# Loading the middle weight columns of a fused q/k/v product as fp32 through SyncE and rounding them on GpSimd

## The chip, the cores and the metric

The kernel runs on one core of one Trainium2 chip. The time is the device time of one execution in microseconds (us); the figure that counts is the median over the runs. Besides the times there is one profiled execution, whose trace gives the start and the duration of every instruction and of the DMA packets.

## The reference

```python
x = np.random.randn(16, 512, 768).astype(np.float32)
w_qkv = np.random.randn(768, 3 * 768).astype(np.float32)

qkv = np.matmul(x, w_qkv)            # (16, 512, 2304)
q, k, v = qkv[..., :768], qkv[..., 768:1536], qkv[..., 1536:]
return np.stack([q, k, v], axis=0)   # (3, 16, 512, 768), fp32
```

So 8192 rows of x, 768 long, are multiplied by one 768 x 2304 matrix w, and the result is written as three matrices.

## The kernel before

**Tiling.** The rows of x are cut into 32 pairs of two 128-row tiles (`p` counts pairs, `r` the row tile in a pair). The columns of w are cut into two groups of 1024 (`q` = 0 and 1), each of two blocks of 512 (`c`), and 256 columns between the groups, the remaining columns (`REM`, at `R_OFF` = 1024). K = 768 is split into six slices `j` of 128, three in each half (`KH` = 3).

**Two ways to multiply.** A pair and a column group make a two by two block product: two row tiles, two halves of K, two column blocks. For most pairs it is done with seven products instead of eight (`do(u, 1)` to `do(u, 7)`, matmuls at L257): products 1 and 2 take bf16 operands (`xb`, `b1`), products 3 to 7 take sums of x blocks (`sums_x`, L224 to L228) and sums of w blocks (`sum_w`, L123) in fp32r. The first two pairs are done in the plain way, in bf16 and slice by slice (`block`, L500), because then PE can begin as soon as the first slices of w are there. The remaining columns are always plain bf16 products against `w_rem[0]` (K slices 0 to 2) and `w_rem[1]` (slices 3 to 5), 128x256 each.

**The order at the start.** The engines' programs are written out by hand (`manual_schedule`): what is called first stands first on its engine. SyncE (SP) issues, in this order, x of pairs 0 and 1, the twelve slices of w for q = 0, the eight parts of x of pair 2 (`load_x_rows(2)`, L141, four for each row tile), and then the blocks of w for q = 1 (`load_blocks(1, 0)` and `(1, 1)`). SP uses eight completion semaphores in turn, so each of its transfers is issued only when the eighth before it has landed. The 256 remaining columns are loaded by GpSimd (POOL): `hold` makes it wait, with a one-element copy, until a slice of w has landed; then it issues two DMAs (L461) that read fp32 and write bf16 into `w_rem[0]` and `w_rem[1]`; a second `hold` waits for pair 2's first row tile.

PE does `block(0, 0)` and `block(0, 1)` for pairs 0 and 1, then `rems_by_halves` (L338, 24 matmuls: both pairs with the first half of `w_rem`, then both pairs with the second half), and then pair 2: products 1 and 2 (L257), the remaining columns of pair 2 (`rem(2)`, L312), products 5 and 6 (`middle`), and from there `block(1, 0)` with products 7, 3 and 4 of pair 2 between its slices.

Pair 2 gets ready as follows. DVE transposes x in four steps (L157), two for each row tile, after it has made the second sum of w blocks (`sum_w(0, 2)`, L123). ACT rounds each row tile to bf16 (`round_row`, L211) among its copies out of PSUM: `late[0]` to `late[3]` (L490) copy the four results of `block(0, 1)`, `rems[...]()` (L327) copy the remaining columns of pairs 0 and 1, `evacuate` (L266) copies product 1. POOL rounds a block of w into `b22[0]` (L581), which product 3 reads. After that ACT rounds w for q = 1 (`cast_j`, L476).

From pair 3 on, each group of pairs repeats the same pattern to the end.

Of the kernel before, what the change touches and what calls it, by code (L numbers as in the profile page):

```python
# [10 lines left out]
def kernel(  # L11
# [20 lines left out]
    nc = tc.nc  # L32
    P = 128
# [5 lines left out]
    KT = K // P  # L39
    KH = KT // 2  # L40
    KC = K // 4
    NP = M // (2 * P)
    CB = 512
    REM = N3 - 4 * CB
    Q_OFF = (0, 2 * CB + REM)
    R_OFF = 2 * CB
    fp32 = mybir.dt.float32
# [3 lines left out]
    add = mybir.AluOpType.add  # L51
# [10 lines left out]
    o_pool = ctx.enter_context(tc.tile_pool(name="o", bufs=5))  # L62
# [9 lines left out]
    ps_pool = ctx.enter_context(tc.tile_pool(name="ps", bufs=8, space=bass.MemoryType.PSUM))  # L72
# [5 lines left out]
    w_rem = [w_pool.tile([P, KH, REM], bf16, name="w_rem0"), None]  # L78
# [13 lines left out]
    def load_w(dst, j0, nj, off, cols):  # L92
        rows = w_qkv.rearrange("(p j) n -> p j n", j=KT)
        nc.sync.dma_start(dst, rows[:, j0:j0 + nj, off:off + cols])  # L94

    stage = {}
# [18 lines left out]
    def sum_w(q, n):  # L115
        t1, t2, t3, t4 = ts[q]
        o, in0, in1 = {
            1: (t1, stage[q, 0, 1], stage[q, 0, 0]),
            2: (t2, stage[q, 1, 1], t1),
            3: (t3, stage[q, 1, 1], stage[q, 0, 1]),  # L120
            4: (t4, stage[q, 1, 0], t2),
        }[n]
        nc.vector.tensor_tensor(o, in0, in1, op=sub)  # L123

    xin, xf, xb, sr = {}, {}, {}, {}
# [8 lines left out]
    def load_x_rows(p, parts=range(8)):  # L134
        if p not in xin:
            xin[p] = xin_pool.tile([P, 2 * P // G, KC], fp32, name="xin")
        rows = x_flat[p * 2 * P:(p + 1) * 2 * P, :].rearrange("(g b) k -> b g k", b=G)
        for n in parts:
            r, i = divmod(n, 4)
            gs = slice(r * P // G, (r + 1) * P // G)  # L140
            nc.sync.dma_start(  # L141
                xin[p][i * G:(i + 1) * G, gs], rows[:, gs, i * KC:(i + 1) * KC]
            )
# [60 lines left out]
    act, dve = nc.scalar, nc.vector  # L204

    def round_row(p, r, eng):
        n = slice(r * P, (r + 1) * P)
        if r == 0:
            xb[p] = xb_pool.tile([P, KT, 2 * P], bf16, name="xb", tag="xb")
        if eng is act:  # L210
            eng.activation(xb[p][:, :, n], xf[p][:, :, n], ident)  # L211
        else:
            eng.tensor_copy(out=xb[p][:, :, n], in_=xf[p][:, :, n])
# [25 lines left out]
    def quad(p, q, pool=o_pool, tag="o"):  # L239
        u = Quad()  # L240
        u.p, u.q = p, q
        u.o = pool.tile([P, 2, 2 * CB], fp32, name="o", tag=tag)
        u.x = u.y = u.z = None
        return u

    def product(u, n, ps, start):
        t1, t2, t3, t4 = ts[u.q]
        if n <= 2:
            h = (n - 1) * KH
            lhs = [xb[u.p][:, h + j, :P] for j in range(KH)]  # L250
            rhs = [b1[u.q][:, h + j, :] for j in range(KH)]
        else:
            k, t = {3: (4, b22[u.q][:]), 4: (0, t4), 5: (1, t1), 6: (2, t2), 7: (3, t3)}[n]
            lhs = [sr[u.p][k][:, j, :] for j in range(KH)]
            rhs = [t[:, j, :] for j in range(KH)]
        for j in range(KH):
            nc.tensor.matmul(  # L257
                ps[:], lhs[j], rhs[j],
                start=(start and j == 0), stop=(j == KH - 1), skip_group_check=True,
            )  # L260

    def bank():
        return ps_pool.tile([P, CB], fp32, name="ps")

    def evacuate(u):
        nc.scalar.activation(u.o[:, 0, :CB], u.x[:], ident)  # L266

    def do(u, n, out=True):
        c11, c12 = u.o[:, 0, :CB], u.o[:, 0, CB:]
        c21, c22 = u.o[:, 1, :CB], u.o[:, 1, CB:]  # L270
        if n == 1:
            u.x = bank()
            product(u, 1, u.x, True)
            if out:
                evacuate(u)
        elif n == 2:
            u.z = bank()
            product(u, 2, u.z, True)
            nc.vector.tensor_tensor(c11, c11, u.z[:], op=add)  # L279
        elif n == 6:  # L280
            product(u, 6, u.x, False)
            nc.scalar.activation(c12, u.x[:], ident)  # L282
        elif n == 5:
            u.y = bank()
            product(u, 5, u.y, True)
        elif n == 7:
            product(u, 7, u.x, False)
            nc.scalar.activation(c22, u.x[:], ident)  # L288
            nc.vector.tensor_tensor(c22, c22, u.y[:], op=add)  # L289
        elif n == 4:  # L290
            product(u, 4, u.x, False)
            nc.scalar.activation(c21, u.x[:], ident)  # L292
        elif n == 3:
            product(u, 3, u.y, False)
            nc.vector.tensor_tensor(c12, c12, u.y[:], op=add)  # L295
# [27 lines left out]
    def rem_copied(p, ps, eng=nc.sync):  # L323

        def copied():
            o = or_pool.tile([P, 2, REM], fp32, name="orem")
            act.activation(o[:], ps[:], ident)  # L327
            return lambda: eng.dma_start(rows_of(1, p, R_OFF - H, R_OFF - H + REM), o[:])

        return copied  # L330

    def rems_by_halves(pairs):
        banks = [ps_pool.tile([P, 2, REM], fp32, name="ps") for _ in pairs]
        for h in range(2):
            for p, ps in zip(pairs, banks):
                for r in range(2):
                    for j in range(KH):
                        nc.tensor.matmul(  # L338
                            ps[:, r, :], xb[p][:, h * KH + j, r * P:(r + 1) * P],
                            w_rem[h][:, j, :], start=(h == 0 and r == 0 and j == 0),  # L340
                            stop=(h == 1 and j == KH - 1), skip_group_check=True,
                        )
        return [rem_copied(p, ps) for p, ps in zip(pairs, banks)]

    def two(a, b, early, ends=(), turns=()):

# [93 lines left out]
    ND = 2  # L440
# [8 lines left out]
    load_row(1, 1)  # L449
    load_slices(0, [(j, 1, 0, CB) for j in range(1, KT)])  # L450
    load_slices(1, [(j, 1, 0, CB) for j in range(KT)])
    load_x_rows(2)

    def hold(src):
        mark = m_pool.tile([P, 1], fp32, name="mark")
        nc.gpsimd.tensor_copy(out=mark[:], in_=src)

    hold(stage[0, 1, 0][:, KH - 1, :1])
    for h in range(2):
        rows = w_qkv.rearrange("(p j) n -> p j n", j=KT)[:, h * KH:(h + 1) * KH]  # L460
        nc.gpsimd.dma_start(w_rem[h][:], rows[:, :, R_OFF:R_OFF + REM])  # L461
    hold(xin[2][:, 0, :1])
    load_blocks(1, 0)

    one = nc.const_aps.tensor(1.0, [P, CB], bf16)
# [16 lines left out]
    def block(q, c, w, groups, between={}):  # L482

        ps = {}
        late = []

        def finish(n):
            p, r = divmod(n, 2)
            u = quads[p, q]
            act.activation(u.o[:, r, c * CB:(c + 1) * CB], ps[n][:], ident)  # L490

        for i, (js, tiles, *cols) in enumerate(groups):
            cols = cols[0] if cols else slice(0, CB)
            for n in tiles:
                p, r = divmod(n, 2)
                fresh = n not in ps
                if fresh:
                    ps[n] = bank()
                for j in js:
                    nc.tensor.matmul(  # L500
                        ps[n][:, cols], xb[p][:, j, r * P:(r + 1) * P], w[:, j, cols],
                        start=(fresh and j == 0), stop=(j == KT - 1), skip_group_check=True,
                    )
                if KT - 1 not in js:
                    continue
                if (p, q) not in quads:
                    quads[p, q] = quad(p, q)
                late.append(lambda n=n: finish(n))
            between.get(i, lambda: None)()
        return late  # L510
# [4 lines left out]
    def copy_y(u):  # L515
        act.activation(u.o[:, 1, CB:], u.y[:], ident)

    def middle(u, order=(6, 5)):
        for n in order:
            do(u, n)  # L520
            if n == 5:
                copy_y(u)
# [51 lines left out]
    for f in late0:  # L574
# [3 lines left out]
    cast_j(0, 1, bt, 4, act)  # L578
    cast_j(0, 1, bt, 5, act)
    sum_w(0, 2)  # L580
    nc.gpsimd.tensor_copy(out=b22[0][:], in_=stage[0, 1, 1])  # L581
    late = block(
        0, 1, bt,
        [((j, ), range(4)) for j in range(KH + 1)] + [(range(KH + 1, KT), range(4))],
    )
    rems = rems_by_halves(range(2))
    transpose(2, 4)

    late[0]()
    late[1]()  # L590
    round_row(2, 0, act)
    rem_stores = [rems[0]()]
    late[2]()
    late[3]()
    round_row(2, 1, act)
    rem_stores.append(rems[1]())
    load_blocks(1, 1)
    for store in rem_stores:
        store()
# [8 lines left out]
    sum_w(0, 3)  # L608
    sums[3](dve)
    sums[4](dve)  # L610

    u = quad(2, 0)
    do(u, 1)
    do(u, 2)
    cast_j(1, 0, b1[1], 0)
    rem2 = rem(2)
    cast_j(1, 0, b1[1], 1)
    middle(u, (5, 6))
    store2 = []

    def rest():
# [126 lines left out]
```

## Time and profile before

| | |
|---|---|
| median of 3 runs | 359.55 us (359.37 to 359.61) |
| the profiled execution, its own time | 359.58 us |
| its span in the trace | 357.7 us |
| busy share of the span | PE 98%, DVE 65%, ACT 52%, POOL 51% |
| DMA | 107.72 MB, mean 301 GB/s over the span |
| DMAs issued by GpSimd | 800 packets, 0.39 MB, both in the first 20 us |

The span runs from the first to the last instruction of the trace; the 1.9 us by which the execution's own time is longer lie around it. In the views, a line such as "18.96 2.62 PE ps L338 x24" gives a start and a length in us, the engine, the tile written, the line of the kernel and the number of instructions. Some matmul records are missing from a trace, so that a group of six can stand as x5. The span that a line gives to a group of matmuls includes the pipeline's run-out of the last one; what one costs is seen from the distance between starts.

### The profile page before, as it was taken

What the parts mean: (1) busy time and instruction counts of PE and PEld (TensorE: products, weight loads), DVE (VectorE), ACT (ScalarE), POOL (GpSimd) and SP (SyncE); (2) the same over time, 40 slices, a digit from 0 to 9 for tenths busy, and PEclk for the clock granted to TensorE, in tenths of its full rate; (3) what the DMA queues carried; (4) which work ended last, traced back from release to release, by engine and by line L of the source; (5) the groups of instructions that cost most, each with busy time, mean ns of one, the idle gap of its engine ahead of it and who ended that gap; (6) DMA issues with size and microseconds to landing.
All of it is one profiled execution on the core that took longest, in us unless ns stands there. A gap on an engine that the chain in (4) does not pass through costs nothing.

```text
span 357.7 us, 5219 instructions
## 1 busy us (share of the span) xinstructions
PE 350.9 (98%) x1755; PEld 253.2 (71%) x1775; DVE 233.1 (65%) x250; ACT 185.1 (52%) x317; POOL 182.6 (51%) x193
## 2 busy tenths in 40 slices
PE   8999999999999999999999999999999999999995
PEld 3465777767768687776867768687776867768774
DVE  3889985887574676647577574676647577544643
ACT  5489545454545454544554545454544554545453
POOL 0228759481754717357371754717357371754420
PEclk9999999999999999999999999999999999999999
DMA  7999999999899898979989899898989989856667
GB/s 284 340 385 333 321 313 406 384 343 328 342 275 339 283 262 324 277 276 309 302 310 247 324 275 339 274 271 331 258 288 316 295 320 239 322 209 234 265 247 254
DMA packets 81963, 107.72 MB, mean 301 GB/s; under 512 B 5264, under 2 KB 62096, under 8 KB 81936
## 3 DMA queue, kind: packets, MB, share of 16 engines
q1 hardware_dynamic: 74288, 101.86, 85.8%
q10 hardware_dynamic: 6848, 5.13, 5.8%
q0 software_dynamic: 800, 0.39, 0.8%
q8 instruction: 14, 0.23, 0.3%
q14 instruction: 13, 0.11, 0.1%
HBM read 32.26 MB, written 75.50 MB: 301 GB/s over the span
## 4 chain that ended last, share of the span: by engine, by line
PE 95%; DMA 1%; ACT 1%; SPq 1%; issue 1%; ACTq 0%; DVE 0%
PE ps L257 79%; PE ps L312 11%; PE ps L500 4%; DMA st<-in_w_qkv_dram 1%; PE ps L338 1%; ACT o L292 1%; SPq L172 0%; ACTq L399 0%; SPq L94 0%; ACT orem L413 0%; ACT both L476 0%; DVE b L478 0%; ACTq L415 0%; ACTq L413 0%
## 5 line engine op out<-in xcount | busy, mean ns | idle before, releaser
L257 PE MATMUL ps<-t,z 128*128 128x512 f32 x366 | 98.3, 390 | 0.0
L257 PE MATMUL ps<-t,s 128*128 128x512 f32 x366 | 97.2, 400 | 0.0
L157 DVE STREAM_TRANSPOSE xf<-xin 128x1536 f32<-128x1536 f32 (+2 forms) x37 | 91.6, 2484 | 2.0 <-DMA xin<-in_x_dram 1.2
L224 POOL TENSOR_TENSOR s<-xf 128x384 fp32r<-128x384 f32 x29 | 29.5, 1018 | 117.9 <-PE ps L257 116.5
L257 PE MATMUL ps<-b,xb 128*128 128x512 bf16 x347 | 83.3, 379 | 1.2
L257 PEld LDWEIGHTS ps<-t,s 128*128 128x128 f32 x366 | 68.7, 188 | 15.9
L257 PEld LDWEIGHTS ps<-t,z 128*128 128x128 f32 x366 | 68.6, 188 | 14.7 <-ACT o L282 0.3
L289 DVE TENSOR_TENSOR o<-o,ps 128x512 f32<-128x512 f32 x56 | 38.4, 685 | 58.7 <-ACT o L288 58.7
L257 PEld LDWEIGHTS <-xb 128*128 128x128 bf16 x366 | 34.3, 98 | 37.5 <-issue 5.0
L279 DVE TENSOR_TENSOR o<-o,ps 128x512 f32<-128x512 f32 x61 | 39.4, 676 | 31.2 <-PE ps L257 28.8
L288 ACT ACTIVATE o<-ps 128x512 f32<-128x512 f32 x56 | 33.5, 598 | 42.7 <-PE ps L257 42.7
L295 DVE TENSOR_TENSOR o<-o,ps 128x512 f32<-128x512 f32 x61 | 41.6, 685 | 20.2 <-PE ps L257 18.9
L282 ACT ACTIVATE o<-ps 128x512 f32<-128x512 f32 x61 | 36.6, 600 | 34.8 <-PE ps L257 32.1
L266 ACT ACTIVATE o<-ps 128x512 f32<-128x512 f32 x61 | 36.4, 598 | 31.3 <-PE ps L257 18.3
L257 PE MATMUL ps<-b,s 128*128 128x512 f32 x183 | 51.2, 390 | 0.0
L292 ACT ACTIVATE o<-ps 128x512 f32<-128x512 f32 x61 | 36.5, 598 | 26.7 <-PE ps L257 23.6
L202 POOL CAST xb<-xf 128x1536 bf16<-128x1536 f32 x28 | 41.0, 1465 | 12.4 <-DVE xf L157 12.4
L312 PE MATMUL ps<-w_rem,xb 128*128 128x256 bf16 x360 | 44.4, 273 | 0.0
L312 PEld LDWEIGHTS <-xb 128*128 128x128 bf16 x360 | 35.0, 98 | 10.8 <-issue 0.5
L257 PEld LDWEIGHTS ps<-b,s 128*128 128x128 f32 x183 | 34.3, 188 | 7.3
L226 POOL TENSOR_TENSOR z<-xf 128x384 fp32r<-128x384 f32 x29 | 29.3, 1011 | 3.9 <-PE ps L257 3.9
L228 POOL TENSOR_TENSOR s<-xf,s 128x384 fp32r<-128x384 f32 x29 | 30.7, 1059 | 0.1
(54 smaller groups left out, 171.3 us busy)
## 6 DMA issues: line engine op xcount, KB each, us to landing
out_dram<-o SPq DMA_DIRECT2D x62, 768.0 KB, 4.6
xin<-in_x_dram SPq DMA_DIRECT2D x90, 192.0 KB, 6.0
out_dram<-o SPq DMA_DIRECT2D x65, 256.0 KB, 3.7
out_dram<-orem SPq DMA_DIRECT2D x31, 256.0 KB, 5.6
xin<-in_x_dram ACTq DMA_DIRECT2D x22, 192.0 KB, 6.7
st<-in_w_qkv_dram SPq DMA_DIRECT2D x11, 256.0 KB, 5.2
st<-in_w_qkv_dram SPq DMA_DIRECT2D x3, 768.0 KB, 10.1
xin<-in_x_dram SPq DMA_DIRECT2D x4, 384.0 KB, 4.2
```

Of the source, the lines that this page charges most:

```text
L157: lambda g=g: nc.vector.transpose(turned[:, g:g + n], rows[:, g:g + n])
L202: nc.gpsimd.tensor_copy(out=xb[p][:], in_=t[:])
L228: 4: lambda g: g.tensor_tensor(s[4], a12, s[2], op=sub),
L257: nc.tensor.matmul(ps[:], lhs[j], rhs[j], start=(start and j == 0), stop=(j == KH - 1), skip_group_check=True,)
L266: nc.scalar.activation(u.o[:, 0, :CB], u.x[:], ident)
L279: nc.vector.tensor_tensor(c11, c11, u.z[:], op=add)
L282: nc.scalar.activation(c12, u.x[:], ident)
L288: nc.scalar.activation(c22, u.x[:], ident)
L289: nc.vector.tensor_tensor(c22, c22, u.y[:], op=add)
L292: nc.scalar.activation(c21, u.x[:], ident)
L295: nc.vector.tensor_tensor(c12, c12, u.y[:], op=add)
L312: nc.tensor.matmul(ps, xb[p][:, j, r * P:(r + 1) * P], w_rem[j // KH][:, j % KH, :], start=(j == 0), stop=(j == KT - 1), skip_group_check= ...
```

## The change

The two DMAs of GpSimd and both of their `hold`s go. A staging tile `st_rem` (128 x 6 x 256 fp32, from the pool of the output tiles, `o`) takes the remaining columns as fp32. SP loads it in two halves, each right behind the four parts of one row tile of pair 2. GpSimd rounds each half into `w_rem` (`round_rem`), the first before and the second behind the rounding into `b22[0]`. On PE the products of pairs 0 and 1 with the remaining columns stand in two parts: those with the first half where they were, those with the second half behind products 1 and 2 of pair 2, which therefore come earlier. ACT copies the remaining columns of both pairs together after `round_row(2, 1)`, and `evacuate` comes ahead of that. `middle(u)` now takes product 6 first and 5 second.

```diff
-    def rems_by_halves(pairs):
-        banks = [ps_pool.tile([P, 2, REM], fp32, name="ps") for _ in pairs]
-        for h in range(2):
-            for p, ps in zip(pairs, banks):
...
+    def rems_half(pairs, banks, h):
+        for p, ps in zip(pairs, banks):
+            for r in range(2):
+                for j in range(KH):
+                    nc.tensor.matmul(
+                        ps[:, r, :], xb[p][:, h * KH + j, r * P:(r + 1) * P],
+                        w_rem[h][:, j, :], start=(h == 0 and r == 0 and j == 0),
+                        stop=(h == 1 and j == KH - 1), skip_group_check=True,
+                    )
...
-    load_x_rows(2)
+    st_rem = o_pool.tile([P, KT, REM], fp32, name="str", tag="o")
+    for h in range(2):
+        n = slice(h * KH, (h + 1) * KH)
+        load_x_rows(2, range(4 * h, 4 * h + 4))
+        load_w(st_rem[:, n], h * KH, KH, R_OFF, REM)
+
+    def round_rem(h):
+        n = slice(h * KH, (h + 1) * KH)
+        nc.gpsimd.tensor_copy(out=w_rem[h][:], in_=st_rem[:, n])
...
-    hold(stage[0, 1, 0][:, KH - 1, :1])
-    for h in range(2):
-        rows = w_qkv.rearrange("(p j) n -> p j n", j=KT)[:, h * KH:(h + 1) * KH]
-        nc.gpsimd.dma_start(w_rem[h][:], rows[:, :, R_OFF:R_OFF + REM])
-    hold(xin[2][:, 0, :1])
     load_blocks(1, 0)
...
     sum_w(0, 2)
+    round_rem(0)
     nc.gpsimd.tensor_copy(out=b22[0][:], in_=stage[0, 1, 1])
+    round_rem(1)
...
-    rems = rems_by_halves(range(2))
+    banks = [ps_pool.tile([P, 2, REM], fp32, name="ps") for _ in range(ND)]
+    rems_half(range(ND), banks, 0)
     transpose(2, 4)
 
     late[0]()
     late[1]()
     round_row(2, 0, act)
-    rem_stores = [rems[0]()]
     late[2]()
     late[3]()
+    u = quad(2, 0)
+    u.x, u.z = bank(), bank()
+    product(u, 1, u.x, True)
+    product(u, 2, u.z, True)
+    rems_half(range(ND), banks, 1)
+    evacuate(u)
     round_row(2, 1, act)
-    rem_stores.append(rems[1]())
+    rem_stores = [rem_copied(p, ps)() for p, ps in enumerate(banks)]
     load_blocks(1, 1)
...
-
-    u = quad(2, 0)
-    do(u, 1)
-    do(u, 2)
+    c11 = u.o[:, 0, :CB]
+    dve.tensor_tensor(c11, c11, u.z[:], op=add)
+
     cast_j(1, 0, b1[1], 0)
     rem2 = rem(2)
     cast_j(1, 0, b1[1], 1)
-    middle(u, (5, 6))
+    middle(u)
```

More of the change, by code (lines that the diff above doesn't have):

```diff
@@ L330, in rem_copied @@
         return copied
-    def rems_by_halves(pairs):
-        banks = [ps_pool.tile([P, 2, REM], fp32, name="ps") for _ in pairs]
-        for h in range(2):
-            for p, ps in zip(pairs, banks):
[L336 to L343, printed above, removed]
+    def rems_half(pairs, banks, h):
[7 more added lines that the diff above has]
+                    )
     def two(a, b, early, ends=(), turns=()):
```

## The prediction

> **What bounds the kernel now.** I read the page's busy times and chain first, then the chain of waits from 9 to 31.5 us, then the instructions of the first 25 us in order of time, and last the DMA by stretches. The first two lines are the page's busy times and its chain by engine.
>
> ```profile
> PE 350.9 (98%) x1755; PEld 253.2 (71%) x1775; DVE 233.1 (65%) x250; ACT 185.1 (52%) x317; POOL 182.6 (51%) x193
> PE 95%; DMA 1%; ACT 1%; SPq 1%; issue 1%; ACTq 0%; DVE 0%
> ```
>
> A busy PE could still be waiting inside its matmuls, so the question is whether the matmuls around the change follow each other at their own pace. The chain of waits (start, length, what) says so:
>
> ```profile
> 11.02 7.93 PE ps L500 x36
> 18.96 2.62 PE ps L338 x24
> 21.58 0.05 issue
> 21.63 1.24 PE ps L257 x5
> 22.87 1.31 PE ps L312 x12
> 24.18 1.39 PE ps L257 x6
> ```
>
> Thirty-six 128x512 bf16 matmuls take 7.93 us, 0.220 each with the run-out of the last; the starts lie 0.216 apart. Twenty-four 128x256 ones take 2.62 us, 0.109 each. The same forms far down the kernel cost the same: 12 of L312 in 1.31 us there too, 0.109 each. So from 9.08 us on PE has no stall that the change could remove. It had none at L338 either: `w_rem` was there in time. The fp32r group behind it costs 0.231 each against 0.227 where it runs on later, 0.08 us over twenty matmuls. That is all that better arrangement could win inside the span.
>
> So the change can only keep PE's line gapless or put gaps into it, and a gap costs its full length, since PE is full up to the end. What decides is whether each operand is there before PE wants it. The engines beside PE (timeline):
>
> ```profile
> 13.09 0.43 DVE L478 CAST both<-st 128x512 bf16<-128x512 f32 x1 [0.22 <-DMA st<-in_w_qkv_dram]
> 15.60 1.76 DVE L123 TENSOR_TENSOR t<-st,t 128x1536 fp32r<-128x1536 f32 x1
> 17.61 1.66 DVE L157 STREAM_TRANSPOSE xf<-xin 128x384 f32<-128x384 f32 x2 [0.26 <-DMA xin<-in_x_dram]
> 17.70 1.09 ACT L490 ACTIVATE o<-ps 128x512 f32<-128x512 f32 x2 [1.43 <-PE ps L500]
> 17.77 1.47 POOL L581 CAST b<-st 128x1536 fp32r<-128x1536 f32 x1
> 18.79 2.78 PE L338 MATMUL ps<-w_rem,xb 128*128 128x256 bf16 x24
> 19.30 0.84 ACT L211 ACTIVATE xb<-xf 128x768 bf16<-128x768 f32 x1 [0.52 <-DVE xf L157]
> 36.97 0.82 POOL L213 CAST xb<-xf 128x768 bf16<-128x768 f32 x1
> ```
>
> And the DMA: stretches of 1 us (last two columns: DMA share, GB/s), GpSimd's queue over 14.5 to 19.5 us, and the stretch from 5.4 to 6.1 us, in which w came as 1 KB packets:
>
> ```profile
> 10.00:11.00 1.00, 0.97 (x5) 0.44 (x5) 0.72 (x2) 0.00 (x0) 0.00 (x0) 1.00 1.02 393
> 14.50:15.00 0.50, 0.50 (x4) 0.26 (x3) 0.50 (x1) 0.50 (x2) 0.00 (x0) 1.00 1.06 350
> 16.00:17.00 1.00, 1.00 (x6) 0.48 (x5) 1.00 (x1) 0.27 (x1) 0.00 (x0) 1.00 1.33 226
> q0 software_dynamic: 800, 0.39, 57.7%
> DMA packets 235, 0.24 MB, mean 338 GB/s; under 512 B 26, under 2 KB 224, under 8 KB 235
> ```
>
> w in 2 KB packets moves at 393 GB/s, x in parts of 768 B at 350; once GpSimd's transfers mix in, the sum falls to 226. GpSimd's 0.39 MB take 57.7% of 5 us, 2.9 us of all engines.
>
> **The change, part by part.**
>
> *Transfers.* Removed: 2.9 us of DMA time for w's columns. Added: twice 128 x 3 rows of 1 KB, 0.393 MB each, at 338 GB/s 1.16 us each, 2.3 us together. A half of x is 0.393 MB too, at 350 GB/s 1.12 us. When do they land? DVE's casts wait for one slice of w after the other; the ninth is there at 13.09 and they come 0.65 apart, so the twelfth lands at about 15.05. The four transfers behind it follow on the one queue: x's first half at 15.05 + 1.12 = 16.17 (before: 17.6, where DVE waited for it), w's first half at 17.33, x's second half at 18.45 (before: about 20.2), w's second half at 19.61. The first block of w for q = 1 is 0.786 MB, 2.0 us at 393, hence at 21.6; its reader, ACT's L476, started at 24.10. SP waits for the eighth transfer back at each issue; w's first half waits for the eleventh slice (14.4), and everything behind it for landings before 17.4, when the queue still holds 2 us of work. Two more issues at 0.43 us delay nothing that is late.
>
> *GpSimd.* Two one-element copies and two DMA issues (1.69 us) go; two roundings of 128x768 come, priced by L213 at 0.82. Round 1 runs from 17.33 to 18.2. PE wants it at 18.79: 0.6 us to spare. Then `b22[0]`, 1.47, to 19.7, against 19.24 before, for a reader (product 3) at 27.1. Round 2: 19.7 to 20.5. What is queued behind the new wait on GpSimd is `b22[0]`, and `z` at L227, which started at 21.86.
>
> [...]
>
> *PE.* No matmul is added or removed. First part at 18.79, 12 x 0.109 = 1.31, to 20.10. Products 1 and 2: 6 x 0.216, to 21.40. Second part (round 2 ready since 20.5) to 22.71. `rem(2)` to 24.02, as before.
>
> *The step that is now early.* Products 1 and 2 move from 21.6 to 20.10, and they need pair 2's first row tile in bf16. With x there at 16.17, DVE is held by `sum_w(0, 2)` alone, to 17.36; transposes to 19.02; ACT is free of L490 at 18.79, so L211 runs 19.05 to 19.9. This is the thinnest cover: 0.2 us. If x did not land earlier at all, L211 would end at 20.14 as before, and PE would wait 0.04.
>
> *ACT behind that.* L490 x2 to 21.0, `evacuate` (product 1 ends at 20.9) to 21.6, L211 of the second row tile to 22.4 (PE wants it at about 23.3, for the second six of `rem(2)`), L327 twice, the second when PE ends its part, to 23.5, two L476 to 24.6. Product 6 ends at about 24.9, its copy at 25.5; product 7 wants it at 26.3. Before, that copy ended at 26.25 and product 7 started at 26.3. That edge gets better, and wins nothing, as PE did not wait.
>
> *Buffers.* The staging tile takes one of five `o` buffers, but every later tile still follows the one five places ahead of it; the tile that follows the staging tile itself, quad (1, 1), comes after 30 us, and round 2 is done at 20.5. PSUM banks are taken in the same order.
>
> The sum: nothing removed from PE's line, nothing added: 359.58 for the profiled execution, which is the median of the runs (359.55) within 0.03. Bounds of the unknown terms: -0.1 us (the fp32r pitch) to +0.3 (thin covers at 20.1 and 18.8 missed by a few tenths). I take 359.6.
>
> **The rivals.**
>
> *GpSimd's first rounding comes late (slower).* PE stands at 18.79 until w's first half is landed and rounded. It decides as soon as the half lands after 18.79 - 0.82 = 17.97, 0.64 later than I have it. For it: the only stretch in which the trace shows these columns moving beside x ran at 226 GB/s. At that rate the x half and the w half take 1.74 us each: landing at 18.53, rounded at 19.35, a gap of 0.56; the second halves land at 22.0, rounded at 22.8, against 21.40 + 0.56, another 0.85. Together 1.4 us: 361.0. Half of that slowing, 360.3. Against it: the slow stretch is the one with GpSimd's queue in it, which is gone, and 1 KB packets on SP's queue made 338. [...]
>
> *The load of w for q = 1 is pushed back.* If DMA time goes by bytes written, the change adds 0.39 MB, 1 us at 393. ACT's L327 for pair 2 started at 29.75, behind a store that waits in the same queue; its casts (L476) end at 31.5, 32.1 and 32.6, and PE wants the three at 32.8, 33.0 and 33.3. One us later costs 0.3: 359.9. Against it: GpSimd's small packets took 2.9 us, more than the 2.3 that come.
>
> *Faster.* It would need a gap that the trace hides, or something in the 1.9 us outside the span that goes with GpSimd's DMAs. No row shows one; if half of that went, 358.7.
>
> **How the numbers follow.** A measurement of this kernel can tell about 0.2%, 0.7 us, from no change. No gap, within 0.1 us: 0.58. Small gaps up to 0.7 us (thin covers, pushed-back loads, a rounding a little late): 0.19. A late rounding or both halves late, over 0.7 us: 0.18. Faster by over 0.7 us: 0.05. So faster 0.05, same 0.77, slower 0.18. The range runs from 359.2, below the fp32r pitch and the spread of the runs, to 360.8, which takes in the smaller half of the late rounding.
>
> **What would show it.** Right: in the timeline after, L338's successor starts at 18.8 and runs 12 in 1.31 us; products 1 and 2 at 20.1; the second twelve at 21.4; GpSimd's casts of 0.8 us start at about 17.4 and 19.7; DVE's first transposes at 17.4 without a wait for DMA. Wrong: a wait of PE for GpSimd at 18.8 or 21.4, or for ACT L211 at 20.1; GpSimd's first cast starting after 18.0; a chain that leaves PE before 30 us. If the span shrinks by more than 0.2 us, my reading that PE had no gap is wrong.

## The result: 0.3% slower, and the profile after

| | changed | before |
|---|---|---|
| median of 14 runs each | 360.89 us (360.23 to 361.71) | 359.66 us (359.37 to 361.53) |
| ratio, 95% interval | 1.003 (1.0018 to 1.0042) | |
| the profiled execution, span | 360.88 us, 359.0 | 359.58 us, 357.7 |

The change costs 1.2 us. The page's busy times and chain hardly differ from before, but DMA now has 5% of the chain where it had 1%, and GpSimd's rounding (L457) stands in it:

```profile
PE 350.3 (98%) x1755; PEld 253.2 (71%) x1775; DVE 232.8 (65%) x250; ACT 185.6 (52%) x317; POOL 182.3 (51%) x191
PE 92%; DMA 5%; ACT 1%; issue 1%; ACTq 0%; POOL 0%; SPq 0%; POOLq 0%
```

The chain of waits of the first 50 us shows one break in PE's line. Before, L338 followed L500 at 18.96; now a chain of transfers and GpSimd's rounding stand in front of L336:

```profile
10.18 6.19 DMA st<-in_w_qkv_dram
16.39 3.10 DMA xin<-in_x_dram
19.53 0.81 POOL w_rem L457
20.38 1.47 PE ps L336 x12
```

The view names `xin` ahead of the rounding, but the rounding reads `st_rem` alone (`str` in the views). In the traces of before and of the changed kernel each transfer reports its landing sixteen times; each report is taken here as that of one of sixteen parts. Those of w's first half came from 17.53 to 19.45, and the rounding, which reads it, started behind the last, at 19.51; ACT's cast of the twelfth slice started at 16.39, behind its last at 16.37. Below, "median landing" is the ninth of the sixteen in order of time, and what the expectations call a lagging ring is a part that lands far behind the others.

The instructions in order of time, with the idle time ahead of each and what ended it:

```profile
16.50 1.76 DVE L123 TENSOR_TENSOR t<-st,t 128x1536 fp32r<-128x1536 f32 x1 [0.65 <-DMA st<-in_w_qkv_dram]
19.51 0.82 POOL L457 CAST w_rem<-str 128x768 bf16<-128x768 f32 x1 [18.21 <-DMA xin<-in_x_dram]
20.38 1.47 PE L336 MATMUL ps<-w_rem,xb 128*128 128x256 bf16 x12 [1.13 <-POOL w_rem L457]
22.04 0.83 POOL L457 CAST w_rem<-str 128x768 bf16<-128x768 f32 x1 [0.29 <-DMA str<-in_w_qkv_dram]
22.98 1.47 PE L336 MATMUL ps<-w_rem,xb 128*128 128x256 bf16 x12
```

GpSimd's first rounding starts at 19.51 and PE starts the first part at 20.38, 1.59 us later than before. Of that, 0.3 was there already where PE's unbroken run begins (9.38 against 9.08); that start moves from one execution to the next, whatever the kernel (8.89 to 9.68 in the profiles of this study). The wait itself is 1.3 us: the start of L336 lies 1.51 behind the last L500, where 0.216 is the pace. PE has no second wait, because the first one gives the second half the time that it needs: rounded at 22.87, wanted at 22.98. Without the first wait, by an estimate from these rows, PE would have waited 0.25 us at product 1 (wanted at 20.40) for ACT's rounding of x, which ended at 20.65, and 0.9 us here. So the later operands are about as late as the first, and the first wait alone is worth little. The spans differ by 1.3 us.

### The profile page after: what moved, and what is told of

Read it like the earlier page. It is cut to its first block, busy times and chain, and to the rows that moved or that the text cites. A ratio compares the mean times of both kernels' runs of the same rounds, so it can differ in the third digit from the quotient of the medians.

```text
span 359.0 us, 5213 instructions
## 1 busy us (share of the span) xinstructions
PE 350.3 (98%) x1755; PEld 253.2 (71%) x1775; DVE 232.8 (65%) x250; ACT 185.6 (52%) x317; POOL 182.3 (51%) x191
## 4 chain that ended last, share of the span: by engine, by line
PE 92%; DMA 5%; ACT 1%; issue 1%; ACTq 0%; POOL 0%; SPq 0%; POOLq 0%
PE ps L257 79%; PE ps L312 11%; DMA st<-in_w_qkv_dram 3%; PE ps L500 1%; DMA touch<-in_w_qkv_dram 1%; DMA xin<-in_x_dram 1%; PE ps L336 1%; ACTq L396 0%; ACT o L292 0%; POOL w_rem L457 0%; ACT orem L410 0%; ACTq L412 0%; SPq L94 0%; POOLq L582 0%; ACTq L410 0%
## 5 line engine op out<-in xcount | busy, mean ns | idle before, releaser
L257 PEld LDWEIGHTS ps<-t,z 128*128 128x128 f32 x366 | 68.6, 188 | 14.4
L312 PE MATMUL ps<-w_rem,xb 128*128 128x256 bf16 x360 | 44.4, 273 | 0.0
L312 PEld LDWEIGHTS <-xb 128*128 128x128 bf16 x360 | 35.1, 98 | 10.5 <-issue 0.5
```

What stands on the lines that cost most here:

```text
L257: nc.tensor.matmul(ps[:], lhs[j], rhs[j], start=(start and j == 0), stop=(j == KH - 1), skip_group_check=True,)
L312: nc.tensor.matmul(ps, xb[p][:, j, r * P:(r + 1) * P], w_rem[j // KH][:, j % KH, :], start=(j == 0), stop=(j == KT - 1), skip_group_check= ...
```

## The experiments

Each ran beside the kernel before on the same chip; they were run in three groups, one chip for each. Two theories stood at the start. A: x's parts, each of which goes into 32 partitions, are slow even without GpSimd's queue (215 GB/s from 15.0 to 15.5 us of the changed kernel), and w's first half stands behind four of them. B: one lagging part of the transfers in that one execution. The rivals for single steps are in the expectations.

**The changed kernel again** (no edit).

> The changed kernel once more, for a second look at the transfers. Theory A (x's parts, which go into 32 partitions each, move at about 217 GB/s even without GpSimd's queue, and w's first half stands behind four of them): PE waits 1.0 to 1.4 us at L336 for GpSimd again, time about 360.9. Theory B (one lagging DMA ring in that one execution made the late landing): PE's wait shrinks to under 0.7 us and the time to under 360.3.

360.95 us, ratio 1.0031 (1.0018 to 1.0044), and again PE waits at L336 for GpSimd:

```profile
PE ps L336 <- POOL w_rem L457: 1.3, 1, 1.3
```

The loss belongs to the kernel, not to one execution. But B is not out: in this trace too the last of the sixteen parts of w's first half lands 2.05 us behind their median (19.89 and 17.84).

**The new order alone.** The loads and `hold`s of before, everything else as changed.

```diff
-    for h in range(2):
-        n = slice(h * KH, (h + 1) * KH)
-        load_x_rows(2, range(4 * h, 4 * h + 4))
-        load_w(st_rem[:, n], h * KH, KH, R_OFF, REM)
...
+    load_x_rows(2)
...
+    hold(stage[0, 1, 0][:, KH - 1, :1])
+    for h in range(2):
+        rows = w_qkv.rearrange("(p j) n -> p j n", j=KT)[:, h * KH:(h + 1) * KH]
+        nc.gpsimd.dma_start(w_rem[h][:], rows[:, :, R_OFF:R_OFF + REM])
+    hold(xin[2][:, 0, :1])
...
-    round_rem(0)
...
-    round_rem(1)
```

> The new order on PE and ACT alone; w's remaining columns come by GpSimd's casting DMAs as before. Theory A (the loads are the whole loss): no wait of PE over 0.1 us, time 359.6 to 359.8. Rival (the order itself costs, since products 1 and 2 come 1.3 us earlier and ACT's copies shift): a gap at product 1 and a time over 360.2.

359.68 us, ratio 1.0 (0.9992 to 1.0009). PE's only wait in the changed part is 0.2 us, for ACT's rounding of the first row tile, which ends at 20.05; the first part at 18.60 and the second at 21.41 wait for nothing:

```profile
18.60 1.47 PE L336 MATMUL ps<-w_rem,xb 128*128 128x256 bf16 x12
19.21 0.84 ACT L211 ACTIVATE xb<-xf 128x768 bf16<-128x768 f32 x1 [0.61 <-DVE xf L157]
20.11 1.47 PE L257 MATMUL ps<-b,xb 128*128 128x512 bf16 x6
21.41 1.47 PE L336 MATMUL ps<-w_rem,xb 128*128 128x256 bf16 x12
```

That wait is twice what I had allowed, and below what the times can tell. The order costs nothing that the times show; the loss is in the loads and the roundings that belong to them.

**The new loads alone.** The kernel before with these lines of the change, without GpSimd's DMAs and `hold`s, and with the order of before on PE and ACT.

```diff
-    load_x_rows(2)
...
+        load_x_rows(2, range(4 * h, 4 * h + 4))
+        load_w(st_rem[:, n], h * KH, KH, R_OFF, REM)
...
+    round_rem(0)
     nc.gpsimd.tensor_copy(out=b22[0][:], in_=stage[0, 1, 1])
+    round_rem(1)
```

> The new loads and GpSimd's roundings alone; PE and ACT keep the order of before (all 24 products of the remaining columns in one piece, ahead of products 1 and 2). Theory A: the first wait of PE stays at about 1.3 us, and a second one of about 1.1 us opens in the middle of the 24, where the second half is rounded only at about 22.9; time about 362.0. Rival (the order matters little): time 360.9.

361.91 us, ratio 1.0052 (1.0032 to 1.0071). Two waits for GpSimd, of 1.3 and 1.2 us:

```profile
PE ps L338 <- POOL w_rem L460: 2.5, 2, 1.3
```

So the split of the products in two parts saves about 1 us of what the loads cost: it is the second of these waits that the changed kernel does not have. (By the times alone it is less sure: the two ran on different chips, and their intervals overlap.)

**x into all partitions.** The same bytes, packets and places in the queue, but each of x's eight transfers for the third pair goes into 128 partitions.

```diff
+    def load_wide(p, r):
...
+        row = (2 * p + r) * P
+        for n in range(4):
+            rows = x_flat[row:row + P, n * KC:(n + 1) * KC]
+            nc.sync.dma_start(xin[p][:, 4 * r + n, :], rows)
...
-        load_x_rows(2, range(4 * h, 4 * h + 4))
+        load_wide(2, h)
```

> The changed kernel, but each of the eight transfers of x for the third pair goes into all 128 partitions instead of 32 (same bytes, same number of 768 B packets, same place in the queue; the third pair's x stands in a wrong layout, so its values are not the reference's). Theory A (32 partitions are the slow term): x's half moves in about 1.1 us instead of 1.8, w's first half lands 0.6 to 0.7 us sooner, PE's wait at L336 falls from 1.3 to about 0.6 us, time about 360.2. Theory B (a lagging ring, or the w half itself): wait unchanged at about 1.3 us, time 360.9.

The DMA by stretches; the last two columns are the share of the engines and GB/s. First the changed kernel, then this one:

```profile
14.50:15.00 0.50, 0.50 (x5) 0.21 (x3) 0.50 (x1) 0.50 (x3) 0.00 (x0) 1.00 1.09 361
15.00:15.50 0.50, 0.50 (x4) 0.26 (x3) 0.50 (x2) 0.50 (x3) 0.00 (x0) 1.00 1.16 215
18.00:18.50 0.50, 0.50 (x4) 0.25 (x3) 0.50 (x2) 0.50 (x2) 0.00 (x0) 1.00 1.04 205
```

```profile
14.50:15.00 0.50, 0.50 (x5) 0.21 (x3) 0.50 (x1) 0.50 (x3) 0.00 (x0) 1.00 1.09 361
15.00:15.50 0.50, 0.50 (x4) 0.26 (x3) 0.50 (x3) 0.50 (x3) 0.00 (x0) 1.00 1.04 335
16.50:17.00 0.50, 0.50 (x4) 0.26 (x3) 0.50 (x1) 0.00 (x0) 0.00 (x0) 1.00 1.08 358
```

Nearly all packets of these stretches are x's, except that w's half begins in the wide kernel's second one. Up to 15.0 us, at the start of x, both kernels move 361 GB/s. From there on the DMA engines are full in both by the column of shares (1.04 to 1.16), but they move 205 to 215 GB/s in the one and 335 to 358 in the other. From the median landing of the last slice of w to that of x's first half it took 1.79 us in the changed kernel (14.83 to 16.62) and 1.07 here (14.43 to 15.50). A has its term. The first wait is gone: w's first half is rounded at 17.90, before PE wants it. That is more than A forecast, and not x's doing alone: in this profile the last part of w's first half also landed only 0.42 us behind the median (16.60 and 17.02), where it was 1.62 in the changed kernel. Yet the time is 362.12 us, ratio 1.0068 (1.0041 to 1.0095), by the medians worse than the changed kernel, since a second wait opened (L465 is the rounding here):

```profile
21.38 1.75 DVE L123 TENSOR_TENSOR t<-st 128x1536 fp32r<-128x1536 f32 x1
21.67 2.14 POOL L465 CAST w_rem<-str 128x768 bf16<-128x768 f32 x1 [2.36 <-DMA str<-in_w_qkv_dram]
23.87 1.47 PE L336 MATMUL ps<-w_rem,xb 128*128 128x256 bf16 x12 [2.44 <-POOL w_rem L465]
```

w's second half had a median landing at 19.23, but its last part at 21.62; and GpSimd's rounding, 0.82 for the first half (17.08 to 17.90), took 2.14 beside DVE's difference of two blocks. The next run moves the second of these away, the one after it both.

**The same, with DVE's difference moved.**

```diff
-    sum_w(0, 3)
     sums[3](dve)
     sums[4](dve)
+    sum_w(0, 3)
```

> The kernel with x's transfers into all 128 partitions (the third pair's values are not the reference's), and on DVE the 1.75 us difference of w blocks moved behind two sums of 0.55 us. In the run without that move GpSimd's second rounding took 2.1 us instead of 0.82, beside that difference. If DVE's instructions with two inputs in SBUF hold GpSimd's copy up, the rounding takes at most 1.4 us now, PE's second wait falls by 0.7 us or more, time about 361.2 where 362.1 was measured. If something else stretched it: time still about 362.

360.83 us, ratio 1.0027 (1.0013 to 1.0041): 1.3 us below the run without the move by medians, though the two ran on different chips and their intervals touch. The second rounding took 1.01 us; `z`, behind it, was now the one stretched, 2.03 us where it took 0.83 in the run without the move:

```profile
22.79 1.01 POOL L465 CAST w_rem<-str 128x768 bf16<-128x768 f32 x1 [1.99 <-DMA str<-in_w_qkv_dram]
23.75 2.03 POOL L227 CAST z<-xf 128x384 fp32r<-128x384 f32 x1
23.85 1.36 PE L336 MATMUL ps<-w_rem,xb 128*128 128x256 bf16 x11 [1.65 <-POOL w_rem L465]
```

The wait that is left, 1.65 us, is the landing: median 20.06, last part 22.73. (The profiled execution, 361.85 us, was one of the longest of the twelve.)

**The same x, without the second half's load** (both roundings read the first half).

> The kernel with x's transfers into all 128 partitions, and without the load of the second half of w's remaining columns (both roundings read the first half; the third pair and the remaining columns are not the reference's). If the landing of that second half, with its last DMA ring about 1 us behind the others, and GpSimd's stretched second rounding are all that is left of the loss, PE has no wait over 0.2 us and the time is 359.6 to 359.9. If the new order or the roundings themselves cost something more, it stays over 360.2.

360.02 us, ratio 0.9997 (0.9986 to 1.0008): no difference from before, and PE's line is whole, with the first part at 19.09, products 1 and 2 at 20.40 and the second part at 21.69. The time is 0.1 us above the expected range; the kernel before had 359.81 in this group. With x fast and the second half's landing away, nothing of the loss is left. The second rounding starts at 19.76 here and takes 0.83, beside no difference of DVE, so this run does not tell what each of the two had cost.

**w's half ahead of x's row tile.**

```diff
-        load_x_rows(2, range(4 * h, 4 * h + 4))
         load_w(st_rem[:, n], h * KH, KH, R_OFF, REM)
+        load_x_rows(2, range(4 * h, 4 * h + 4))
```

> The changed kernel with each half of w's remaining columns ahead of the row tile of x instead of behind it. Theory A (the queue holds about 1.3 us more work than PE leaves time for, whoever is last): GpSimd rounds the first half by about 18.2, no wait at L336, but x lands 1.2 us later, ACT L211 ends at about 21.3 and PE waits about 1.0 to 1.4 us at product 1 instead; time 360.6 to 361.1. Theory C (only the rounding on GpSimd is late, and x has slack): the gap goes, time about 359.7.

361.02 us, ratio 1.0036 (1.0024 to 1.0048). As A has it the wait at L336 is gone and the time stays; but PE waited only 0.26 us at product 1. The larger wait is one step on, for the second row tile's rounding on ACT, whose x landed last:

```profile
21.55 1.61 DVE L157 STREAM_TRANSPOSE xf<-xin 128x384 f32<-128x384 f32 x2 [2.17 <-DMA xin<-in_x_dram]
23.20 0.84 ACT L211 ACTIVATE xb<-xf 128x768 bf16<-128x768 f32 x1 [1.43 <-DVE xf L157]
24.10 0.83 PE L312 MATMUL ps<-w_rem,xb 128*128 128x256 bf16 x6 [0.35 <-ACT xb L211]
```

The execution that was profiled is the shortest of this kernel's eight (360.29 us; the longest was 361.75), so these waits are smaller than usual.

**w's halves in ACT's queue,** beside x's parts:

```diff
-        load_w(st_rem[:, n], h * KH, KH, R_OFF, REM)
...
     for f in late0:
         f()
+    for h in range(2):
+        rows = w_qkv.rearrange("(p j) n -> p j n", j=KT)[:, h * KH:(h + 1) * KH]
+        nc.scalar.dma_start(st_rem[:, h * KH:(h + 1) * KH], rows[:, :, R_OFF:R_OFF + REM])
```

> The changed kernel, but the two halves of w's remaining columns are issued by ACT, behind its four copies of the first block, so that they lie in another queue beside x's parts instead of behind them. Theory A (x's parts leave half of the path into memory unused, and a transfer into all partitions can fill it, as GpSimd's DMAs did before): the two move together at over 300 GB/s, the first half is rounded about 0.7 to 1.2 us sooner, PE's wait at L336 is under 0.6 us, time 359.7 to 360.2. Rival (the engines are simply full): no sooner landing, time 360.9.

Half of it came: w was there sooner. From the median landing of the twelfth slice to the last part of w's first half it took 3.5 us (14.68 to 18.18) where the changed kernel took 4.6 (14.83 to 19.45), to that of the second half 5.3 where it took 7.1, and the wait at L336 falls to 0.24 us. The time doesn't fall: 360.74 us, ratio 1.0029 (1.0015 to 1.0043). Here x's second row tile is late (its last part at 22.06, 7.4 us after the twelfth slice's median landing) and `rem(2)` waits for ACT. So x and w together were there no sooner than in the changed kernel:

```profile
PE ps L312 <- ACT xb L211: 0.8, 1, 0.8
```

**The first rounding in three pieces.**

```diff
+        if h == 0:
+            for j in range(KH):
+                nc.gpsimd.tensor_copy(out=w_rem[0][:, j, :], in_=st_rem[:, j, :])
+            return
         nc.gpsimd.tensor_copy(out=w_rem[h][:], in_=st_rem[:, n])
```

> The changed kernel with the first rounding on GpSimd cut into three of 256 columns, one for each K slice. If the rounding's own 0.82 us is on the path, PE starts L336 after the first piece, 0.4 to 0.5 us sooner, and the time falls to about 360.4. If PE waits for something else (the landing is late by itself, but PE's next wait takes over, for instance ACT L211 or the later pieces), the gap is only split and the time stays within 0.2 of 360.9.

360.83 us, ratio 1.0029 (1.0014 to 1.0043). PE starts L336 0.45 us after GpSimd's first piece (18.90 and 19.35), and then waits 0.8 us for the second half:

```profile
PE ps L336 <- POOL w_rem L461: 0.8, 1, 0.8
```

The second alternative of the expectation holds: the gap is split, and behind the first half stands the landing of the second. What the pieces save does not show here. In this profile w's first half landed early, 3.7 us after the twelfth slice's median (15.18 to 18.85) where the changed kernel took 4.6, and the twelve products took 1.94 us instead of 1.47, since PE also waits for the second and the third piece (its weight loads go on at 19.69 and 20.04).

**x's parts in two queues** (the two into partitions 64 to 127 of each row tile issued by ACT).

```diff
-        load_x_rows(2, range(4 * h, 4 * h + 4))
+        load_x_rows(2, range(4 * h, 4 * h + 2))
...
+    load_x_rows(2, (2, 3), nc.scalar)
     for f in late0:
         f()
+    load_x_rows(2, (6, 7), nc.scalar)
```

> The changed kernel, but of the four transfers of each row tile of x for the third pair, the last two (partitions 64 to 127) are issued by ACT, so that they can move beside the first two (partitions 0 to 63) instead of behind them. Theory A (x is slow because one transfer reaches 32 partitions only, and two such transfers into different partitions go well together): x's half moves in about 1.1 to 1.3 us, PE's first wait falls from 1.3 to 0.5 to 0.8 us; ACT's four issues cost its copies 0.9 us where it has time. Time 360.0 to 360.6. Rival (two queues do not add up): first wait 1.2 us or more, time 360.9 or more.

361.38 us, ratio 1.0037 (1.0026 to 1.0049): a miss, and no test of A. ACT's transfers started ahead of the last slices of w instead of beside x's other parts. The twelfth slice landed last at 17.28 (16.37 in the changed kernel), `block(0, 1)` itself waited 0.5 us for ACT's cast, and w's first half came no sooner (rounding at 19.48).

## Why the prediction was right or wrong

The forecast of 359.6 us was wrong: it rested on a PE line without a gap, and PE got one. What came is the first rival, GpSimd's first rounding late, to which I gave a chance of 0.18. That its 361.0 lies 0.1 us from the measured 360.89 is in part luck. It was two waits, 0.56 and 0.85, with x's half and w's half both at 226 GB/s and no late parts; what came was one wait of 1.3 us, with x's half at that pace (1.79 us for 1.74), w's half faster (1.21) and the last parts late. The time lies 0.1 us above the range's upper end, which was that high for the smaller half of this rival.

- *PE is full, a gap costs its length.* Right: one wait of 1.3 us, and a loss of 1.2 by the medians.
- *PE's sum, the early products, ACT behind that, buffers.* Right but for a small cover: the new order alone took 359.68 us, and PE waited 0.2 us at product 1, where I had 0.04 for an x that lands no earlier.
- *GpSimd's price.* Right: 0.82 and 0.83 us measured, 0.82 predicted from L213. What was missing: beside a 1.75 us instruction of DVE on blocks of w (L123) the same rounding took 2.14 us in the run with x into all partitions and 1.48 in the one with w ahead (below).
- *Landings.* Here the step failed. For w's halves I had 17.33 and 19.61; their last parts landed at 19.45 and 21.98. The half of x was sized at 1.12 us, from a stretch of 350 GB/s, and took 1.79 between medians. That stretch (14.5 to 15.0) does hold x's packets, 217 of 768 B beside 4 of 2 KB. But it is the start of x's transfers, in which narrow and wide ones move alike (361 GB/s in both kernels above). The pace of the narrow ones drops behind it, to 215 from 15.0 to 15.5 us, and in the trace of before GpSimd's DMAs begin at that moment (first packet at 15.02, 231 GB/s in the same stretch) and hide it. w's half itself was sized rightly, 1.16 against 1.21 between medians.

```profile
DMA packets 252, 0.17 MB, mean 350 GB/s; under 512 B 31, under 2 KB 248, under 8 KB 252
```

- *The slow row.* The 226 GB/s (before, 16 to 17) are the sum of both queues, GpSimd's q0 with more bytes than x in q1. That x alone moves at 205 to 215 without that queue is another figure, and near it by coincidence.

```profile
q0 software_dynamic: 264, 0.13, 94.3%
q1 hardware_dynamic: 141, 0.10, 38.9%
```

- *The tail of a landing.* By its median w's first half was there at 17.83, 0.5 after my 17.33: x's 0.67 and w's 0.05 more, less 0.22 by which the twelfth slice's median came ahead of my 15.05. The other 1.62 us of the 2.1 is how far the last of sixteen parts landed behind that median. My step had no such term: it took landings 0.65 apart from DVE's waits, and added the bytes. The tail is older than the new loads' landings: the last part of the twelfth slice landed at 16.37, 1.54 behind its median; before, it landed at 15.47, 0.56 behind, and not at my 15.05.
- *The eighth transfer back.* I let w's first half wait for the eleventh slice, at 14.4. Eight back is the ninth slice, whose last part landed at 13.39; the half was issued at 13.41. Nothing hung on it.
- *What GpSimd's DMAs cost.* I counted the removal of 2.9 us of engine time as a gain. But in the trace of before x and w's columns, 1.57 MB read in all, were both there 5.2 us after the twelfth slice's median landing (14.91 to 20.10). One behind the other in SP's queue they took 7.1 (14.83 to 21.98). About half of that difference is the tail: to the last median landing it is 4.8 and 5.8. No run tells whether GpSimd's DMAs were cheaper because they ran beside x or because they write half as many bytes.
- *The other rivals.* Neither the load of w for q = 1 nor anything outside the span decided: PE waits for neither, and the time outside the span is 1.9 us in both profiles.

What stays open is why a part falls behind, and with it how much of the 1.2 us is x's pace and how much the tail. In the profiles of the changed kernel and its variants the last part of x's and w's transfers lands 0.4 to 2.7 us behind the median, on different transfers each time. No run took that away.

## What to carry to other kernels

Size a transfer from a stretch that is long enough: the start of x moved at 361 GB/s whatever its form, the next half microsecond at 215 or 335, by the partitions that it reached. Where two queues share a stretch, look at the bytes of each before you take the sum for the pace of one. The engine time of the transfers that you remove is not what their removal wins: here 2.9 us of it went, and x and w took 7.1 us to land where they had taken 5.2. A landing was that of the last of sixteen parts, 0.4 to 2.7 us behind the median: give it a microsecond or more of cover. And when four operands come through one queue expect that moving one ahead hands the wait to another, as it did with w ahead (0.35 us at L312) and with w in ACT's queue (0.8 us).

## What the runs showed of the hardware

**Into 32 partitions x moved at little more than half the pace.** At their start (14.5 to 15.0 us) the 768-byte packets moved at 361 GB/s in both forms; behind it at 205 to 215 into 32 partitions and at 335 to 358 into 128, with the engines shown as full in both (1.04 to 1.16). What makes the difference, no trace shows. Nor does a run show that x's parts leave half of a path unused which a transfer into all partitions can fill, as theory A had it for the run with w in ACT's queue: there w's second half was there 5.3 us after the twelfth slice's median landing instead of 7.1, and x's second row tile 7.4 us after it instead of 6.0 (14.83 to 20.83).

**Beside DVE's work on blocks of w GpSimd's rounding took longer.** The same rounding took 0.82 us, 2.14 beside DVE's 1.75 us difference of two blocks (L123), 1.01 when that was moved away, and 1.48 in the run with w ahead, where it started beside another instruction of L123:

```profile
16.34 1.48 POOL L457 CAST w_rem<-str 128x768 bf16<-128x768 f32 x1 [15.04 <-DMA str<-in_w_qkv_dram]
```

In both the rounding started second and ended shortly behind DVE's instruction, with most of its usual time between the two ends: that instruction ended at 21.38 + 1.75 = 23.13, and the rounding 0.68 later, at 23.81; in the run with w ahead it is 15.38 + 1.75 = 17.13, and 0.69 to the rounding's end at 17.82. It went the other way too: where the rounding was first (22.79, the run with the difference moved), the difference, at 23.03, took 2.38 us instead of 1.75.

**A transfer of instructions fell into the same stretch.** One packet of 16 KB in a queue that the trace calls instruction took 1.25 us (2.6% of sixteen engines over 18 to 21 us of the changed kernel), in the very stretch in which the landings decide:

```profile
q8 instruction: 1, 0.02, 2.6%
```

It may be part of a tail. In seven of the twelve profiles, that of before among them, the last of the sixteen parts fell 0.8 to 1.7 us further behind the fifteenth at a transfer that landed next after this packet (before: from 0.06 to 1.40 us, the packet at 20.28 to 21.35). In one run the same fall came ahead of the packet. And it does not explain the first wait of the changed kernel: there the last part was late from the twelfth slice on, at 16.37 and, in the second profile, 16.86, and the packet began at 18.92 and 19.00.
